# Products of zeros at the start, parameter loads on one queue, an earlier copy of the shift columns and a root on VectorE, in a one-layer decoder step

## The chip, the cores and the metric

One core of a Trainium2 chip runs the whole step. The metric is the device time of one execution in microseconds (us); the median of three runs counts. TensorE multiplies matrices, VectorE (DVE), ScalarE (ACT) and GpSimd (POOL) work on elements, and SyncE (SP) issues most of the transfers from and to device memory (HBM). Each engine takes its own instructions in order, and so does each queue of transfers.

## The reference, cut to what matters

One layer is computed for 512 prompt tokens and 8 sample tokens, 1024 wide, all in f32:

```
mod = silu(c) @ w_mod + b_mod              # six parts: sh1, sc1, g1, sh2, sc2, g2
h   = rmsnorm(x, norm1_g) * (1 + sc1) + sh1
u   = h @ w_in                             # q, f, i (v), output gate, x and y of the recurrence, two merge gates
o   = rmsnorm(hgrn2(q, f, v), hg_onorm_g) * silu(output gate)      # 8 heads of 128
b   = rglru(conv(x)) * gelu(y)
x   = x + g1 * ((sig(ga) * (o @ w_branch_a) + sig(gb) * (b @ w_branch_b)) @ w_out)
x   = x + g2 * (relu((rmsnorm(x, norm2_g) * (1 + sc2) + sh2) @ w_ff1) ** 2 @ w_ff2)
y   = rmsnorm(x, final_norm_g)
```

The prompt tokens share one conditioning vector; each of the 8 samples has its own, so there are 9 columns of `mod`. For the samples the recurrences take one step from stored states. The last two old inputs of the convolution (`state_conv`) are handed through to an output.

## The kernel before, in words

Activations lie transposed: 128 features in the partitions, 520 tokens (512 and 8) in the free dimension, cut into two halves of 260. A product of f32 precision is made of three products of the type fp32r: each operand is split into a high part (a cast on ScalarE) and a low part (a subtraction on VectorE), and TensorE adds high by high, high by low and low by high. A tile of weights is 128 columns by 1024 rows (512 KB); SP loads it (`_load_w`, L100), ScalarE casts `whi` (L113), VectorE subtracts `wlo` (L116), and for each of 8 blocks of rows TensorE makes six products of 128x260 (`gemm`, L155). Every two records of the trace on a plain f32 operand belong to one instruction.

**The opening** (`begin`, L1668) is written by hand, and a wrapper, `InOrder`, keeps TensorE, ScalarE and VectorE in the order of the code; its operations all show as L72. `load_parameters` (L254) loads `pm` (b_mod and norm gains) and `pl` (bounds and decays) by ScalarE's queue and `pa` (convolution, gate biases and old states, and the norm gain of the heads) by GpSimd's; the samples `xsr` come by ScalarE's queue too. SP loads, in this order, the conditioning `c`, the first quarter ("piece 0") of the part of `w_mod` that makes the scale sc1, x rows 0 and 1, two weight tiles, piece 1, x rows 2 and 3, the third weight tile, x rows 4 to 7, pieces 2 and 3, and then `w_rows`, the part of `w_mod` that makes the shift sh1. Each piece is multiplied by silu(c) (`pt<-wm,cT`), evicted by ScalarE (`modev`), turned into columns (`pt<-pick,modev`), and its two rows of h, still without norm and shift, are cast (`h`, high on ScalarE, low on VectorE) and multiplied by the first three tiles (f, q and output gate of head 0; `fhi`, `flo`). Meanwhile the squares of x are summed for the norm's root `rs`.

Near the end of the opening the shift columns `shp` are there. h is cast again, now with norm and shift: `high_again` and `low_again`, eight each. The three tiles that are already multiplied get the shift afterwards: `pw` is the product of `shp` with the raw weights (L1893, `pb<-wst,shp`), ScalarE copies it to `sw` (`shw<-pb`), three small products (`pt<-pick,shw`) turn it into the column `bias`, VectorE copies that to `shb`, and ScalarE and VectorE add it to the three evicted results `ma`. `evict(2)` multiplies the third result by `rs`. Behind this stands the first ordinary tile, v of head 0 (`gemm`, which is tied behind the three small products by `last_product`).

**After the opening** a scheduler orders each engine by a simulated timeline, priorities and tied pairs (`behind`). Heads, recurrences and gates follow, all fed by the h of the opening.

**The gates** come after eight plain tiles: products of sums of quarter matrices (`gate_product`, L874, products on L897), whose weights are split into `wgate` four forms ahead (L870, L871); results go to `gp` by a copy on ScalarE (L908). The same stretch holds the end of the heads. `heads_sample_out` (L669) normalizes the samples' heads: a product sums squares over the partitions, ScalarE copies it (L676), and `root` (L213) on GpSimd adds a constant and raises to the power -0.5; VectorE multiplies `os` by it (L678). GpSimd's queue also stores the last two heads' outputs (`oaT_d<-e`, L666) and loads gate weights (`gw`, L853) and the recurrences' outputs (`t<-obT_d`, L788). `load_ob` (L780) splits those `t` into `b` (cast on ScalarE L209, subtraction on VectorE L210).

Of the kernel before, what the change touches and what calls it, by code (L numbers as in the profile page):

```python
# [17 lines left out]
NB = 8  # L18
T = L + NB
HALF = T // 2  # L20
KO = D // 128
H = 8
# [3 lines left out]
EPS = 1e-6  # L26
# [8 lines left out]
FIRSTS = 3  # L35
# [44 lines left out]
class Kernel:  # L80
# [126 lines left out]
    def split(self, full, pool, tag):  # L207
# [2 lines left out]
        self.nc.vector.tensor_tensor(lo, full, hi.bitcast(F32), OP.subtract)  # L210
        return hi, lo

    def root(self, out, x, n):  # L213

        p = self.nc.gpsimd
        p.tensor_scalar(out, x, n * EPS, None, OP.add)  # L216
        p.tensor_tensor(out, out, self.halfc.to_broadcast(list(out.shape)), OP.pow)
# [36 lines left out]
    def load_parameters(self):  # L254

        self.pm = self.consts.tile([128, 72], F32, name="pm")
        self.nc.scalar.dma_start(self.pm, self.i["params_mod"])
        self.bmod, self.n1g, self.n2g = self.pm[:, 0:48], self.pm[:, 48:56], self.pm[:, 56:64]
        self.gcol = self.pm[:, 70:72]
        self.pl = self.start.tile([128, 16], F32, name="pl")  # L260
        self.nc.scalar.dma_start(self.pl, self.i["params_bound"])
        t = self.hc.tile([128, 313], F32, name="pa")
        self.nc.gpsimd.dma_start(t, self.i["params"])
        self.ong = self.hc.tile([128, 1], F32, name="ong")
        self.nc.gpsimd.tensor_scalar(self.ong, t[:, 0:1], 128.0 ** 0.5, None, OP.mult)
        self.cw = t[:, 1:33].rearrange("p (j k) -> p j k", j=4)
        self.cb, self.ba, self.bx = (t[:, 33 + 8 * j:41 + 8 * j] for j in range(3))
        self.h0 = t[:, 57:121].rearrange("p (b k) -> p b k", b=NB)
        self.cbuf = t[:, 121:313].rearrange("p (b j k) -> p b j k", b=NB, j=3)
# [399 lines left out]
    def heads_sample_out(self):  # L669
        nc = self.nc  # L670
        sq = self.sm.tile([128, H * NB], F32, name="sq64")
        osf = self.os.rearrange("p h b -> p (h b)")
        nc.scalar.activation(sq, osf, AF.Square)
        ps = self.pps.tile([128, 512], F32, name="ps")
        nc.tensor.matmul(ps[:, :64], self.ones_r.bitcast(F32), sq, start=True, stop=True)
        nc.scalar.copy(sq, ps[:, :64])  # L676
        self.root(sq, sq, 128)
        nc.vector.tensor_tensor(osf, osf, sq, OP.mult)  # L678
        nc.vector.tensor_tensor(osf, osf, self.ogs.rearrange("p h b -> p (h b)"), OP.mult)

# [92 lines left out]
    def rg_out(self):  # L773
        nc, o = self.nc, self.o
        nc.gpsimd.dma_start(o["xlast"], self.xlast.rearrange("p n w -> p (n w)"))
        nc.gpsimd.dma_start(o["hlast"], self.hlast.rearrange("p n w -> p (n w)"))
        nc.gpsimd.dma_start(o["conv_old"], self.i["state_conv"][0, :, 1:3])


    def load_ob(self):  # L780
# [887 lines left out]
    def begin(self):  # L1668


        plain = self.nc
        nc = self.nc = InOrder(self.tc)
        self.start = self.open_pool("start", 1)
        mm = lambda: self.pmm.tile([128, 2, 512], F32, name="mm")
        ps = lambda: self.pps.tile([128, 512], F32, name="ps")
        pt = lambda: self.ppt.tile([128, 512], F32, name="pt")
        pb = lambda: self.ppb.tile([128, 512], F32, name="pb")
        self.load_c()
        self.load_parameters()
        xsr, fs, fsh = (self.start.tile([128, KO, NB], F32, name=n) for n in ("xsr", "fs", "fsh"))  # L1680
        nc.scalar.dma_start(xsr.rearrange("p k b -> p (k b)"), self.i["xs"])
        self.xT = [self.slot(self.start, f"xT{k}", bufs=1) for k in range(KO)]
        keys, raw, pieces = [self.head_cols(0)[j] for j in (0, 1, 3)], [], []

        def load_wide(name, i):
            w = self.start.tile([128, KO, 256], F32, name="wm", bufs=4)
            nc.sync.dma_start(w.rearrange("p k n -> p (k n)"), self.i[name][i])
            return w

        def load_piece(i):  # L1690
            pieces.append(load_wide("w_piece", i))

        load_piece(0)
        self.load_x(0, 1)
        for key in keys[:2]:
            raw.append(self._load_w(key, self.wst))
        load_piece(1)
        self.load_x(2, 3)
        raw.append(self._load_w(keys[2], self.wst))
        self.load_x(4, 5, 6, 7)  # L1700
        load_piece(2)
        load_piece(3)

# [121 lines left out]
        p = self.piece(1, pieces[1])  # L1825
# [15 lines left out]
        p = self.piece(2, pieces[2])  # L1841
# [8 lines left out]
        rs = self.slot(self.start, "rs", bufs=1)  # L1850
# [3 lines left out]
        p = self.piece(3, pieces[3])  # L1854
# [29 lines left out]
        products(2, 6, 7, only=high_part)  # L1884
        self.mod_cols(0, self.shp[:, :, :NM], ev)
        products(2, 6, 7, only=low_parts)
        for i in range(KO // 2):
            high_again(2 * i, 2 * i + 1)
            low_again(2 * i, 2 * i + 1)
            samples_again(i)  # L1890
            if i == 0:
                evict(2)
        pw = pb()  # L1893
        for n in range(FIRSTS):
            for k in range(KO):
                r = 32 * (k % 4)
                nc.tensor.matmul(pw[r:r + 32, n * 128:(n + 1) * 128], self.shp[:, k, :], raw[n][:, k, :],
                                 start=k < 4, stop=k >= KO - 4)
        sw, b = self.start.tile([128, FIRSTS * 128], F32, name="shw"), self.start.tile([128, FIRSTS, 16], F32, name="shb")
        nc.scalar.copy(sw, pw[:, :FIRSTS * 128])  # L1900
        bias = pt()
        for n in range(FIRSTS):
# [4 lines left out]
            nc.scalar.activation(u[:, :L], u[:, :L], AF.Identity, bias=b[:, n, 0:1])  # L1907
            nc.vector.tensor_tensor(u[:, L:], u[:, L:], b[:, n, 1:9], OP.add)
        self.first = [self.two(u) for u in us]
        self.last_product = nc.tensor.last  # L1910
        self.nc = plain
        self.close_pool()
        nc = plain
# [144 lines left out]
```

## Time and profile before

| | |
|---|---|
| median of 3 runs | 1016.55 us (1015.34 to 1017.27) |
| the profiled execution | 1017.95 us, its span 1016.2 us |
| busy: TensorE, VectorE, ScalarE, GpSimd | 97%, 68%, 52%, 14% of the span |
| HBM read, written | 123.65 MB, 11.26 MB |

Times in the views are microseconds from the start of the span. A row of the timeline gives the start, the length, the engine (PE is TensorE's products, PEld its weight loads, a q behind a name its queue), the line, the operation, out<-in, shapes and count, and in brackets the idle time before it with what ended it. A row of the waits gives who waited for whom, the microseconds in total, how often, and the longest. A row of the windows gives the stretch, its length, the busy time of PE, PEld, DVE, ACT and POOL with their counts, the clock that TensorE was granted (1.00 is full), the busy share of the transfer engines and GB/s.

### The profile page before, as it was taken

What the parts mean: (1) busy time and instruction counts of PE and PEld (TensorE: products, weight loads), DVE (VectorE), ACT (ScalarE), POOL (GpSimd) and SP (SyncE); (2) the same over time, 40 slices, a digit from 0 to 9 for tenths busy, and PEclk for the clock granted to TensorE, in tenths of its full rate; (3) what the DMA queues carried; (4) which work ended last, traced back from release to release, by engine and by line L of the source; (5) the groups of instructions that cost most, each with busy time, mean ns of one, the idle gap of its engine ahead of it and who ended that gap; (6) DMA issues with size and microseconds to landing.
All of it is one profiled execution on the core that took longest, in us unless ns stands there. A gap on an engine that the chain in (4) does not pass through costs nothing. (4 is left out here: it accounts for less than half of the span.)

```text
span 1016.2 us, 23148 instructions
## 1 busy us (share of the span) xinstructions
PE 986.3 (97%) x9624; PEld 956.5 (94%) x9624; DVE 689.2 (68%) x1344; ACT 525.9 (52%) x998; POOL 146.3 (14%) x250
## 2 busy tenths in 40 slices
PE   6899999999999999979999999999999999999997
PEld 4799999999989999979999999999999999999996
DVE  6776766685685758858624546677767776778685
ACT  5554745725564573455512224466555645656662
POOL 1300000000000101161000000022321331232050
PEclk9989999999999999999999999999999999999998
DMA  9553353233234335335556665321662472273242
GB/s 364 199 180 115 114 163 116 103 126 128 97 126 154 113 100 197 109 106 199 175 203 243 225 244 187 97 91 48 152 176 63 97 197 102 55 179 80 64 84 85
DMA packets 48761, 143.67 MB, mean 141 GB/s; under 512 B 6240, under 2 KB 15776, under 8 KB 47624
## 3 DMA queue, kind: packets, MB, share of 16 engines
q1 hardware_dynamic: 36704, 123.23, 35.6%
q0 software_dynamic: 11504, 18.86, 8.3%
q8 instruction: 75, 1.23, 0.5%
q10 hardware_dynamic: 448, 0.11, 0.1%
q14 instruction: 30, 0.25, 0.1%
HBM read 123.65 MB, written 11.26 MB: 133 GB/s over the span
## 5 line engine op out<-in xcount | busy, mean ns | idle before, releaser
L155 PE MATMUL mm<-h,whi 128*128 128x260 f32 (+1 forms) x2720 | 453.1, 285 | 0.0
L155 PEld LDWEIGHTS mm<-h,whi 128*128 128x128 f32 x2720 | 380.0, 189 | 1.4 <-issue 0.8
L155 PE MATMUL mm<-h,wlo 128*128 128x260 f32 x1360 | 280.7, 286 | 2.6 <-DVE wlo L116 2.6
L116 DVE TENSOR_TENSOR wlo<-wst,whi 128x1024 fp32r<-128x1024 f32 x156 | 190.2, 1220 | 126.5 <-ACT whi L113 125.2
L113 ACT CAST whi<-wst 128x1024 fp32r<-128x1024 f32 x156 | 164.0, 1053 | 185.2 <-PE mm L155 145.0
L155 PEld LDWEIGHTS mm<-h,wlo 128*128 128x128 f32 x1360 | 213.0, 189 | 3.7 <-DVE wlo L116 3.2
L1280 POOL TENSOR_TENSOR ft<-ft,fsh 128x8 f32<-128x8 f32 x28 | 18.4, 658 | 209.2 <-DVE ft L1274 209.2
L1288 DVE TENSOR_TENSOR f<-f 128x260 f32<-128x260 f32 x64 | 27.3, 426 | 27.9 <-ACT f L1283 27.2
L1277 ACT ACTIVATE ft<-ft,fsh 128x512 f32<-128x512 f32 (+2 forms) x36 | 24.1, 678 | 36.0 <-DVE ft L1274 36.0
L155 PE MATMUL mm<-oa,whi 128*128 128x260 f32 x256 | 41.6, 284 | 0.0
L155 PE MATMUL mm<-b,whi 128*128 128x260 f32 x256 | 41.6, 284 | 0.0
L155 PE MATMUL mm<-a,whi 128*128 128x260 f32 x256 | 41.4, 284 | 0.0
L569 DVE TENSOR_TENSOR X<-X,tb 128x512 f32<-128x512 f32 x48 | 30.8, 680 | 11.0 <-PE ps L561 8.6
L216 POOL TENSOR_SCALAR ss<-ss 128x4 f32<-128x4 f32 x8 | 2.4, 304 | 246.7 <-ACT g L653 246.6
L155 PEld LDWEIGHTS mm<-oa,whi 128*128 128x128 f32 x256 | 34.8, 188 | 2.1 <-ACT whi L113 1.6
L155 PEld LDWEIGHTS mm<-b,whi 128*128 128x128 f32 x256 | 35.1, 188 | 1.7 <-ACT whi L113 1.2
L155 PEld LDWEIGHTS mm<-a,whi 128*128 128x128 f32 x256 | 35.0, 188 | 1.2 <-PE pt L346 0.8
L179 ACT ACTIVATE gate<-pb,pa 128x260 f32<-128x260 f32 x32 | 15.5, 486 | 32.1 <-PE pb L701 32.1
L1322 POOL DMA_DIRECT2D ma<-snap x28 | 26.4, 956 | 39.2 <-issue 30.7
L1304 POOL DMA_DIRECT2D ma<-snap x28 | 26.1, 932 | 39.2 <-DMA ma<-snap 23.8
L871 DVE TENSOR_TENSOR wgate<-gw,wgate 128x512 fp32r<-128x512 f32 x28 | 19.2, 690 | 15.0 <-ACT wgate L870 14.3
L1283 ACT ACTIVATE f<-ft 128x520 f32<-128x520 f32 (+1 forms) x36 | 20.8, 589 | 14.9 <-POOL ft L1281 12.9
(560 smaller groups left out, 2083.2 us busy)
## 6 DMA issues: line engine op xcount, KB each, us to landing
wst<-in_w_ff_dram SPq DMA_DIRECT2D x64, 512.0 KB, 3.9
wst<-in_w_in_dram SPq DMA_DIRECT2D x56, 512.0 KB, 3.5
wst<-in_w_mod_dram SPq DMA_DIRECT2D x32, 512.0 KB, 4.4
wm<-in_w_piece_dram SPq DMA_DIRECT2D x4, 1024.0 KB
wm<-in_w_rows_dram SPq DMA_DIRECT2D x4, 1024.0 KB, 12.0
st<-in_state_hgrn_dram SPq DMA_DIRECT2D x8, 512.0 KB, 4.1
vb<-vd SPq DMA_DIRECT2D x8, 512.0 KB, 3.7
out_dram<-st SPq DMA_DIRECT2D x8, 512.0 KB
```

The lines of the kernel that those rows point to most:

```text
L113: ins = self.nc.scalar.copy(hi, st)
L116: self.nc.vector.tensor_tensor(lo, st, hi.bitcast(F32), OP.subtract)
L155: self.last_product = self.nc.tensor.matmul(ps[s][:, :c.stop - c.start], x, y[:, c], start=first and n == 0, stop=last and n == 2)
L179: ins = self.nc.scalar.activation(out, x, AF.Sigmoid, **kw)
L569: last = nc.vector.tensor_tensor(half, half, factors(tbs, x, b), OP.mult)
L871: nc.vector.tensor_tensor(lo, x, hi.bitcast(F32), OP.subtract)
L1277: nc.scalar.activation(t[:, :p], t[:, :p], AF.Relu, bias=sh[:, 0:1])
L1280: eng.tensor_tensor(t[:, p:], t[:, p:], sh[:, 1:9], OP.add)
L1283: nc.scalar.activation(f, self.two(self.ft)[:, a:a + n], AF.Square)
L1288: self.nc.vector.tensor_tensor(f[:, n], f[:, a], f[:, b], op)
L1304: nc.gpsimd.dma_start(x[1][:, b], v[:, :n], accum_op=OP.add)
L1322: nc.gpsimd.dma_start(x[t][:, a], s[p], accum_op=OP.add)
```

## The change

- Six f32 products of zeros (`shp`, just cleared) stand ahead of piece 0 on TensorE.
- `pm`, `pl` and `xsr` are issued by SP (the first two ahead of piece 0, `xsr` behind x row 1), and `pa` too, between x row 7 and piece 2. `ong`, which reads `pa`, is computed later in the code. The copy of `state_conv` to an output stands behind a late product instead of in the opening.
- The copy to `sw` stands behind the fourth `high_again` instead of behind the eighth; `evict(2)` stands behind all of them. The small products, `shb` and the additions are outside the wrapper now, and v's tile is tied to the last product of `pw`, not to the small ones.
- The samples' root is computed by VectorE: an integer estimate and three Newton steps, 12 operations, and one that reads the sum straight from PSUM.

```
     def load_parameters(self):
-        self.nc.scalar.dma_start(self.pm, self.i["params_mod"])
+        self.nc.sync.dma_start(self.pm, self.i["params_mod"])
...
-        nc.scalar.copy(sq, ps[:, :64])
-        self.root(sq, sq, 128)
+        nc.vector.tensor_scalar(sq, ps[:, :64], 128 * EPS, None, OP.add)
+        sq = self.rsqrt_small(sq, H * NB, w=H * NB)
...
+    def rsqrt_small(self, x, n, p=128, w=16):
...
+        nc.vector.tensor_scalar(t.bitcast(I32), x.bitcast(I32), 1, None, OP.arith_shift_right)
+        nc.vector.tensor_scalar(y.bitcast(I32), t.bitcast(I32), -1.0, float(0x5F3759DF), OP.mult, OP.add)
+        nc.vector.tensor_scalar(h, x, -0.5, None, OP.mult)
+        for _ in range(3):
+            nc.vector.tensor_tensor(t, y, y, OP.mult)
+            nc.vector.tensor_tensor(t, t, h, OP.mult)
+            nc.vector.scalar_tensor_tensor(y, t, 1.5, y, OP.add, OP.mult)
...
-        nc.gpsimd.dma_start(o["conv_old"], self.i["state_conv"][0, :, 1:3])
+        self.behind(nc.gpsimd.dma_start(o["conv_old"], self.i["state_conv"][0, :, 1:3]), self.last_product)
...
         self.load_parameters()
+        warm = pb()
+        for _ in range(6):
+            nc.tensor.matmul(warm[:, :256], self.shp[:, :4, :], self.shp, start=True, stop=True)
...
         self.load_x(4, 5, 6, 7)
+        nc.sync.dma_start(self.pa, self.i["params"])
         load_piece(2)
...
-        for i in range(KO // 2):
-            high_again(2 * i, 2 * i + 1)
-            low_again(2 * i, 2 * i + 1)
-            samples_again(i)
-            if i == 0:
-                evict(2)
         pw = pb()
...
-        nc.scalar.copy(sw, pw[:, :FIRSTS * 128])
+        for i in range(KO // 2):
+            high_again(2 * i, 2 * i + 1)
+            low_again(2 * i, 2 * i + 1)
+            samples_again(i)
+            if i == 1:
+                nc.scalar.copy(sw, pw[:, :FIRSTS * 128])
+        evict(2)
+        self.last_product = nc.tensor.last
+        self.nc = nc = plain
         bias = pt()
+        nc.gpsimd.tensor_scalar(self.ong, self.pa[:, 0:1], 128.0 ** 0.5, None, OP.mult)
...
-        self.last_product = nc.tensor.last
-        self.nc = plain
         self.close_pool()
```

On TensorE, at the end of the opening, the product of the shift with the raw weights (`pb<-wst,shp`) was followed by the three small products and then by v's tile (`whi` and `wlo` rows):

```order
L72 MATMUL pb<-wst,shp 32x128 x24
L72 MATMUL pt<-pick,shw 128x9 x3
L155 MATMUL mm<-h,whi 128x260 x4
L155 MATMUL mm<-h,wlo 128x260 x2
L155 MATMUL mm<-h,whi 128x260 x4
L155 MATMUL mm<-h,wlo 128x260 x2
```

Now it is followed by v's tile at once:

```order
L72 MATMUL pb<-wst,shp 32x128 x24
L155 MATMUL mm<-h,whi 128x260 x4
L155 MATMUL mm<-h,wlo 128x260 x2
L155 MATMUL mm<-h,whi 128x260 x4
L155 MATMUL mm<-h,wlo 128x260 x2
L155 MATMUL mm<-h,whi 128x260 x4
L155 MATMUL mm<-h,wlo 128x260 x2
L155 MATMUL mm<-h,whi 128x260 x2
L1923 MATMUL pt<-pick,shw 128x9 x3
L155 MATMUL mm<-h,whi 128x260 x2
L155 MATMUL mm<-h,wlo 128x260 x2
```

The three small products moved into the fourth of v's eight blocks. On ScalarE the same place read, before (`h<-xT,shp` are the casts of `high_again`, `whi` the second ordinary tile's high part, `ma` the additions of the bias):

```order
L72 ACTIVATE h<-xT_124,shp 128x512
L72 ACTIVATE h<-xT_125,shp 128x512
L72 ACTIVATE h<-xT_126,shp 128x512
L72 ACTIVATE h<-xT_127,shp 128x512
L72 ACTIVATE h<-xT_128,shp 128x512
L113 CAST whi<-wst 128x1024
L72 COPY shw<-pb 128x384
L72 ACTIVATE ma<-ma,shb 128x512 x3
```

and reads now:

```order
L72 ACTIVATE h<-xT_128,shp 128x512
L72 COPY shw<-pb 128x384
L72 ACTIVATE h<-xT_129,shp 128x512
L72 ACTIVATE h<-xT_130,shp 128x512
L72 ACTIVATE h<-xT_131,shp 128x512
L72 ACTIVATE h<-xT_132,shp 128x512
L113 CAST whi<-wst 128x1024
L1927 ACTIVATE ma<-ma,shb 128x512 x3
```

The copy of the shift moved ahead of four casts and of `whi`. On ScalarE at the first gates, where `gp` are results of gate products and `b` the recurrences' outputs, the order before was

```order
L870 CAST wgate<-gw 128x512 x3
L908 COPY gp<-mm 128x260
L908 COPY gp<-ps 128x260
L209 CAST b<-t 128x520 x4
L908 COPY gp<-mm 128x260
L870 CAST wgate<-gw 128x512
```

and is now

```order
L883 CAST wgate<-gw 128x512 x3
L921 COPY gp<-mm 128x260
L921 COPY gp<-ps 128x260
L209 CAST b<-t 128x520 x3
L921 COPY gp<-mm 128x260
L883 CAST wgate<-gw 128x512
L209 CAST b<-t 128x520
```

The fourth cast of `b` moved behind the third copy to `gp`; the copy to `sq` for the root is gone from ScalarE, and the two operations of the root are gone from GpSimd.

More of the change, by code (lines that the diff above doesn't have):

```diff
@@ L211, in split @@
         return hi, lo
+    def rsqrt_small(self, x, n, p=128, w=16):
+        nc = self.nc
+        y, t, h = (self.sm.tile([128, w], F32, name=f"rs{w}_{a}", bufs=2 if w == 16 else 1) for a in "yth")
+        y, t, h = y[:p, :n], t[:p, :n], h[:p, :n]
+        nc.vector.tensor_scalar(t.bitcast(I32), x.bitcast(I32), 1, None, OP.arith_shift_right)
[5 more added lines that the diff above has]
+            nc.vector.scalar_tensor_tensor(y, t, 1.5, y, OP.add, OP.mult)
+        return y
     def root(self, out, x, n):
@@ L260, in load_parameters @@
         self.pl = self.start.tile([128, 16], F32, name="pl")
-        self.nc.scalar.dma_start(self.pl, self.i["params_bound"])
-        t = self.hc.tile([128, 313], F32, name="pa")
-        self.nc.gpsimd.dma_start(t, self.i["params"])
+        self.nc.sync.dma_start(self.pl, self.i["params_bound"])
+        self.pa = t = self.hc.tile([128, 313], F32, name="pa")
         self.ong = self.hc.tile([128, 1], F32, name="ong")
-        self.nc.gpsimd.tensor_scalar(self.ong, t[:, 0:1], 128.0 ** 0.5, None, OP.mult)
         self.cw = t[:, 1:33].rearrange("p (j k) -> p j k", j=4)
@@ L1679, in begin @@
         self.load_parameters()
+        warm = pb()
+        for _ in range(6):
+            nc.tensor.matmul(warm[:, :256], self.shp[:, :4, :], self.shp, start=True, stop=True)
         xsr, fs, fsh = (self.start.tile([128, KO, NB], F32, name=n) for n in ("xsr", "fs", "fsh"))
-        nc.scalar.dma_start(xsr.rearrange("p k b -> p (k b)"), self.i["xs"])
         self.xT = [self.slot(self.start, f"xT{k}", bufs=1) for k in range(KO)]
@@ L1694, in begin @@
         self.load_x(0, 1)
+        nc.sync.dma_start(xsr.rearrange("p k b -> p (k b)"), self.i["xs"])
         for key in keys[:2]:
@@ L1899, in begin @@
         sw, b = self.start.tile([128, FIRSTS * 128], F32, name="shw"), self.start.tile([128, FIRSTS, 16], F32, name="shb")
-        nc.scalar.copy(sw, pw[:, :FIRSTS * 128])
+        for i in range(KO // 2):
[7 more added lines that the diff above has]
+        self.nc = nc = plain
         bias = pt()
-        for n in range(FIRSTS):
+        nc.gpsimd.tensor_scalar(self.ong, self.pa[:, 0:1], 128.0 ** 0.5, None, OP.mult)
+        for n, u in enumerate(us):
             nc.tensor.matmul(bias[:, 16 * n:16 * n + NM], sw[:, n * 128:(n + 1) * 128], self.pick[:, :NM], start=True,
@@ L1909, in begin @@
         self.first = [self.two(u) for u in us]
-        self.last_product = nc.tensor.last
-        self.nc = plain
         self.close_pool()
-        nc = plain
         pool = lambda name, **kw: self.tc.tile_pool(name=name, bufs=2, reuse_waits="tile", **kw)
```

## The prediction, made before the changed kernel had run

> **What bounds the kernel now.** TensorE is the bound: the page has it busy for 97% of the span, so I first asked the waits of TensorE what it waited for, up to 52 us and behind that:
>
> ```profile
> PE pt L72 <- DMA wm<-in_w_piece_dram: 6.9, 1, 6.9
> PE pt L72 <- ACT shw L72: 4.2, 1, 4.2
> ...
> PE mm L897 <- ACT gp L908: 5.5, 2, 4.4
> PE mm L155 <- DVE wlo L116: 2.6, 3, 0.9
> ```
>
> Three waits matter: for the first piece, for the copy of the shift (`shw`) and for a gate copy (`gp`). The change touches each of them. Then I asked the windows for the granted clock around them:
>
> ```profile
> 12.18:15.60 3.42, 3.12 (x12) 2.68 (x12) 3.42 (x4) 2.44 (x4) 0.00 (x0) 1.00 1.00 392
> 46.32:49.73 3.41, 0.95 (x36) 0.68 (x28) 3.41 (x7) 3.41 (x7) 3.06 (x8) 1.00 0.59 173
> 53.14:56.56 3.42, 3.42 (x17) 3.42 (x17) 1.19 (x6) 3.36 (x6) 0.00 (x0) 0.50 0.65 229
> 56.56:60.00 3.44, 3.44 (x31) 3.44 (x30) 3.44 (x14) 2.67 (x9) 0.00 (x0) 1.00 0.83 314
> 298.86:302.27 3.41, 2.48 (x21) 2.33 (x20) 3.41 (x7) 2.50 (x4) 0.00 (x0) 1.00 0.66 197
> 455.95:459.36 3.41, 3.41 (x24) 1.91 (x23) 2.79 (x6) 3.41 (x7) 0.26 (x1) 0.50 0.46 125
> 1005.50:1008.90 3.40, 2.34 (x18) 2.16 (x18) 2.53 (x13) 1.10 (x3) 0.41 (x2) 1.00 0.27 94
> 1008.90:1012.00 3.10, 1.22 (x12) 0.75 (x10) 2.25 (x6) 1.55 (x3) 0.00 (x0) 0.50 0.48 190
> ```
>
> The clock changes only at these borders, which lie a multiple of 3.41 us apart. It falls to 0.50 behind a window in which TensorE was busy for 0.95 of 3.41 us or 2.34 of 3.40, and stays at 1.00 through one of 2.48 of 3.41; so the limit is near 70% busy. It comes back behind a window that was busy throughout. A wait of 4 us therefore costs twice: itself, and half of the work up to the next border but one.
>
> **Products of zeros, and the parameters.** The timeline of the opening:
>
> ```profile
> 6.92 1.93 PE L72 MATMUL pt<-wm,cT 128*32 128x256 f32 x16 [6.92 <-DMA wm<-in_w_piece_dram]
> 7.00 0.17 DVE L72 COPY ptmp<-pl 128x8 f32<-128x8 f32 x1 [2.76 <-DMA pl<-in_params_bound_dram]
> 9.93 1.05 ACT L72 CAST fhi<-wst 128x1024 fp32r<-128x1024 f32 x1 [0.26 <-DMA wst<-in_w_in_dram]
> 11.28 1.34 ACT L72 ACTIVATE h<-xT,modT 128x512 fp32r<-128x512 f32 x2 [0.30 <-DVE modT L72]
> 12.05 2.28 PE L72 MATMUL mm<-h,fhi 128*128 128x260 f32 x8 [1.31 <-ACT h L72]
> 14.64 1.24 PE L72 MATMUL mm<-h,flo 128*128 128x260 f32 x4 [0.30 <-DVE flo L72]
> 20.28 1.12 PE L72 MATMUL ps<-h,fhi 128*128 128x260 f32 x8
> 24.95 1.07 PE L72 MATMUL pt<-wm,cT 128*32 128x256 f32 x16
> 27.71 0.22 POOL L72 TENSOR_TENSOR fs<-xsr,modT 128x16 f32<-128x16 f32 x1 [5.29 <-DVE modT L72]
> 33.88 1.05 PE L72 MATMUL pb<-rsd,ones_r 128*128 128x128 f32 x8
> ```
>
> The first windows are marked 1.00, but the same eight products last 2.28 us at 12.05 and 1.12 at 20.28, and a piece 1.93 and 1.07: the opening runs at half speed. The window up to 15.60 (3.12 of 3.42 us busy) did not end that; the one up to 19.01 did.
>
> Cost of the six: four f32 products of 128 columns take 1.05 us at full speed, 0.26 each, so one of 256 columns takes 0.26 to 0.53, at half speed 0.53 to 1.05, six 3.2 to 6.3 us. `shp` is cleared at about 1.4 us, so they end between 4.6 and 7.7 us, beside the wait for piece 0. I take no cost; the latest end would cost 0.8 us, were it not for the next point.
>
> Gain: `pm` and `pl` go ahead of piece 0 on SP, each one issue (some 0.4 us), so piece 0 comes up to 0.8 us later; `pa`, `xsr` and the state copy no longer run beside it, which gives part of that back. I take 7.3 us. `pl` came at 7.00 and had held VectorE for 2.76 us; it now comes before piece 0, and ScalarE's exponentials and table load with it. But next in line on ScalarE is the cast of `fhi`, which waits at 9.93 for its tile, whose bytes are no fewer ahead of it. So h starts at 11.0 instead of 11.28, and the first real products at 11.8 instead of 12.05: 0.25 us. Between piece 0 (over at 8.4 if at full speed) and 11.8 TensorE has only the two column products, half a microsecond. Every 3.41 us window that covers this hole is busy for 55% at most, under the 70% limit, wherever its borders fall. So even if the six products lift the clock, I expect it to lapse before the stream, and to come back near 19 us as before, give or take half a window of 3.41 us at half speed, 0.9 us. The term is -0.2, bounds -2.1 (clock held: the chain reaches 14.4 us on ScalarE and VectorE as before, and from there 4.6 us to 19.0 run at full speed, less 0.2 for waits) and +0.9.
>
> [...]
>
> `pa` now lies between x row 7 and piece 2. Its reader `ong` stands on GpSimd ahead of the sample step of 27.71. Piece 2, next behind it, was in use at 24.95 with no wait shown, so `pa` is there in time; if not, each microsecond past 27.7 delays the samples' columns of h and TensorE alike. I take 0. The state copy moves to a stretch behind the gates where GpSimd only issues loads: 0.
>
> **The shift.** The timeline there:
>
> ```profile
> 45.10 5.03 ACT L72 ACTIVATE h<-xT,shp 128x512 fp32r<-128x512 f32 x8 [0.99 <-DVE shp L72]
> 45.76 1.52 PE L72 MATMUL pb<-wst,shp 128*32 128x128 f32 x48
> 47.20 0.76 DVE L72 TENSOR_TENSOR ma<-ps,rs 128x260 f32<-128x260 f32 x2
> 47.87 4.06 DVE L72 SCALAR_TENSOR_TENSOR h<-xT,shp,h 128x512 fp32r<-128x512 f32 x6
> 50.97 0.47 ACT L72 COPY shw<-pb 128x384 f32<-128x384 f32 x1
> 51.49 1.45 PE L72 MATMUL pt<-pick,shw 128*128 128x9 f32 x6 [4.22 <-ACT shw L72]
> 52.79 1.21 PE L155 MATMUL mm<-h,whi 128*128 128x260 f32 x4
> 58.16 0.65 PE L155 MATMUL mm<-h,whi 128*128 128x260 f32 x4
> 58.88 0.65 PE L155 MATMUL mm<-h,whi 128*128 128x260 f32 x4
> 60.33 0.65 PE L155 MATMUL mm<-h,whi 128*128 128x260 f32 x4
> ```
>
> TensorE is through with `pw` at 47.28, waits 4.2 us for a copy behind eight casts, does the small products (51.49 to 52.79) and v's eight blocks (to 60.33, the next tile), up to 56.56 at half speed: 13.05 us. Now v follows at once. A block takes 0.72 us at full speed (58.16 to 58.88), eight 5.76; the small products half of 1.30, 0.65; together 6.4, to 53.7 us. What is late next: block k needs `low_again` k. VectorE goes on at 47.28 with rows 2 to 7 at 0.68 each, `evict(2)` (0.76) now behind them; ScalarE has a cast each 0.63, 0.47 later from row 4 on. So row 2 is ready at 47.9, needed at 48.7; row 7, behind `shb`, at 51.7, needed at 53.0. The second tile's `whi` ends near 51.6; its `wlo` (1.2 us, behind `evict(2)`) near 53.9, as it is needed. The third tile's `whi` stands behind the bias and four sigmoid passes, near 57, its `wlo` near 60.2 for 60.0. I charge 0.3 for that. Gain 13.05 - 6.4 - 0.3 = 6.3; bounds 4 (each of these ends a microsecond later) and 6.7.
>
> **The samples' root.** GpSimd, ScalarE, VectorE and TensorE at the gates:
>
> ```profile
> 438.46 10.55 POOL L217 TENSOR_TENSOR sq<-sq,halfc 128x64 f32<-128x64 f32 x1
> 448.96 1.18 POOL L666 DMA_DIRECT2D oaT_d<-e  x2
> ...
> 446.20 1.69 ACT L209 CAST b<-t 128x520 fp32r<-128x520 f32 x3
> 452.73 0.63 ACT L209 CAST b<-t 128x520 fp32r<-128x520 f32 x1 [4.83 <-DMA oaT_d<-e]
> 453.26 0.37 ACT L908 COPY gp<-mm 128x260 f32<-128x260 f32 x1
> ...
> 441.71 0.69 DVE L665 TENSOR_TENSOR e<-pb,e 128x512 f32<-128x512 f32 x1 [0.47 <-PE pb L663]
> 449.05 0.23 DVE L678 TENSOR_TENSOR os<-os,sq 128x64 f32<-128x64 f32 x1 [2.56 <-POOL sq L217]
> ...
> 447.63 1.61 PE L897 MATMUL pb<-h,wgate 128*128 128x260 f32 x12
> 453.68 2.97 PE L897 MATMUL mm<-a,wgate 128*128 128x260 f32 x12 [4.45 <-ACT gp L908]
> ```
>
> The power takes 10.55 us on GpSimd. Behind it wait the stores of `e`, issued at 448.96 though `e` was ready at 442.4; ScalarE's fourth `b` waits for them until 452.73 (`b` takes over that memory), and behind `b` stands the copy to `gp` for which TensorE waits 4.45 us. Then it runs at half speed from 453.68 to 459.36: another 2.84. Together 7.3.
>
> Now VectorE has 13 operations on 128x64; `os` shows 0.23 for one, so 3.0 us, among the `wgate` splits and ahead of the second `e`. If all of it delayed that `e`, it would end at 445.4, the stores go out then, and 3.8 us later (448.96 to 452.73, as before) the fourth `b` can start. That `b` now stands behind the `gp` copy, which comes after three casts of `b`, at 447.9 + 0.4 = 448.3, before TensorE ends its product at 449.24. So the wait goes. What is late next is the loads of the fifth and sixth `t` ahead of a later copy on ScalarE; I charge 0.5. Gain 6.8; bounds 2.5 (a wait over 1 us remains and the clock falls again) and 7.3.
>
> **The sum.** -0.2 - 6.3 - 6.8 = -13.3 us. Against the profiled execution (1017.95, span 1016.2 and 1.75 around it) that is 1004.65. The median of the runs is 1016.55, 1.4 lower, and their spread of 1.9 us is what borders 3.41 us apart would make of three slow stretches; so I put the sum on the median: 1003.2.
>
> **Rivals.** (1) The clock holds across the hole of the opening. For it: the six products fill the time up to piece 0. Against it: the 70% limit. Then -2.1 for -0.2: 1001.3. [...] Chance 0.12.
>
> (2) The gate wait shrinks but stays over 1 us, with ScalarE behind the later `t` loads, and the clock falls again: 1 to 2 us and 2.8. For it: ScalarE takes everything in one order and a fifth `t` needs the buffer of the first. Against it: TensorE needs that later copy only some 8 us after. 1003.2 + 4.3 = 1007.5. Chance 0.20.
>
> (3) Slower: up to the second pair of heads the order of all engines is laid out anew, over some 20 tiles, and `wlo` comes late for them, since ScalarE and VectorE lose the slack that TensorE's wait for `shw` had given them. Its price is the longest such wait, 0.9 us a tile. It decides from 15 tiles on (13.3 / 0.9); all 20 give 1003.2 + 18.0 = 1021.2. Against it: before, only three waits on `wlo` are shown behind 52 us, 2.6 us. Chance 0.03.
>
> (4) The gains are eaten further on by transfers that come no sooner than before, and nothing is left: 1016.5. Against it: of TensorE's waits the views show only the first piece's as one for a load. Chance 0.02.
>
> My forecast has the remaining 0.63: 1003.2, its own range 1001.5 to 1005.5. The range that leaves out about 2 in 10 goes from 1000.5 (rival 1 with 0.8 for the borders) to 1008 (rival 2). A measurement here tells 0.2%, 2 us, from no change: faster 0.95, within 0.2% 0.02, slower 0.03.
>
> **What would show it.** Right: no wait of TensorE on `shw`, v's first `whi` right behind `pb<-wst,shp`, the clock at 1.00 from there to the gates, no power on GpSimd at 64 columns, no wait over 1 us on L921's `gp`. The opening: eight `h,fhi` products of about 2.3 us mean it lapsed, 1.1 that it held. Wrong: a new wait of TensorE over 1 us anywhere behind 50 us, or a window under 70% busy there.

## The result and the profile after

The changed kernel takes 1006.66 us in the median of four runs (1005.01 to 1007.33), the kernel before 1016.91 us beside it (1015.34 to 1017.46): ratio 0.9899, 95% interval 0.9882 to 0.9916. That is 10.2 us faster, where the forecast had 13.3 us and 1003.2 us; the time lies in the range, near the price of rival 2 (1007.5). The profiled execution took 1007.33 us, its span 1005.5 us; against 1016.2 us before, 10.7 us less. The 2.6 us between 13.3 and 10.7 are what had to be found.

The waits of TensorE in the changed kernel, up to 52 us and behind that (who waited for whom: us in total, times, longest):

```profile
PE mm L72 <- ACT h L72: 2.2, 1, 2.2
PE pb L72 <- DVE shp L72: 1.5, 1, 1.5
PE pt L72 <- DVE ptmp L325: 1.0, 1, 1.0
...
PE mm L155 <- DVE wlo L116: 2.6, 3, 1.0
PE mm L72 <- DVE ma L72: 1.2, 1, 1.2
PE mm L910 <- DVE wgate L884: 1.2, 1, 1.2
PE mm L910 <- ACT gp L921: 1.0, 1, 1.0
PE mm L910 <- ACT wgate L883: 1.0, 1, 1.0
```

The waits on `shw` (4.2 us) and the long one on `gp` (4.4 us) are gone. What is new are two waits on `wgate`, the split gate weights: 1.0 us for ScalarE's cast and 1.2 us for VectorE's subtraction. The wait of 1.0 us on `gp` is the smaller of the two that stood there before. The windows around the half-speed stretches of the changed kernel (length, busy time of PE, PEld, DVE, ACT, POOL, clock, share of the transfer engines, GB/s):

```profile
7.29:10.70 3.41, 1.68 (x20) 1.02 (x20) 1.24 (x8) 0.50 (x2) 0.01 (x1) 1.00 1.05 419
10.70:14.12 3.42, 1.82 (x7) 1.72 (x8) 1.84 (x3) 3.42 (x5) 0.62 (x3) 0.50 1.01 409
14.12:17.53 3.41, 3.10 (x23) 1.68 (x21) 2.45 (x3) 0.74 (x2) 0.00 (x0) 0.50 1.04 398
451.02:454.44 3.42, 1.81 (x12) 1.59 (x13) 2.68 (x5) 1.14 (x3) 0.53 (x1) 1.00 0.02 5
454.44:457.85 3.41, 3.41 (x18) 3.41 (x17) 1.23 (x3) 1.43 (x4) 0.00 (x0) 0.50 0.49 154
```

The clock lapses in the opening's hole and comes back at 17.5 us; from there it stays at 1.00 through the shift and up to 454.4 us, and falls at the gates, behind the window that holds the two waits on `wgate`. (Near the end of the kernel it falls at 1000.6 us, as it did at 1008.9 us before.)

To see where the time went, the span is cut at three places that every trace has: the start of the shift product (`pb<-wst,shp`), the first gate product (`mm<-h,wgate`) and the first product of `b` (`mm<-b,whi`). These are the rows of TensorE's timeline in the changed kernel:

```profile
45.32 1.52 PE L72 MATMUL pb<-wst,shp 128*32 128x128 f32 x48
46.77 0.74 PE L155 MATMUL mm<-h,whi 128*128 128x260 f32 x4
434.79 1.60 PE L910 MATMUL mm<-h,wgate 128*128 128x260 f32 x12
484.05 0.40 PE L155 MATMUL mm<-b,whi 128*128 128x260 f32 x2
```

And in the kernel before, whose shift product starts at 45.76 us (a row of the prediction):

```profile
441.99 1.62 PE L897 MATMUL mm<-h,wgate 128*128 128x260 f32 x12
460.39 3.04 PE L897 MATMUL mm<-h,wgate 128*128 128x260 f32 x24
494.40 0.40 PE L155 MATMUL mm<-b,whi 128*128 128x260 f32 x2
```

| | before | after | difference | forecast |
|---|---|---|---|---|
| opening, to the shift product | 45.76 | 45.32 | -0.44 | -0.2 |
| shift and heads, to the first gate product | 396.23 | 389.47 | -6.76 | -6.3 |
| gates, to the first product of `b` | 52.41 | 49.26 | -3.15 | -6.8 |
| rest, to the end of the span | 521.80 | 521.45 | -0.35 | 0 |

The difference is in one term: the gates. TensorE's rows there, in the changed kernel:

```profile
445.92 3.04 PE L910 MATMUL mm<-h,wgate 128*128 128x260 f32 x24
448.80 1.61 PE L910 MATMUL ps<-a,wgate 128*128 128x260 f32 x12
451.42 0.52 PE L910 MATMUL mm<-a,wgate 128*128 128x260 f32 x2 [1.00 <-ACT wgate L883]
453.15 1.53 PE L910 MATMUL mm<-a,wgate 128*128 128x260 f32 x10 [1.22 <-DVE wgate L884]
454.48 2.80 PE L910 MATMUL pb<-h,wgate 128*128 128x260 f32 x12
```

The same `x24` row, at 445.92 us here, starts at 460.39 us in the kernel before. So up to here the change had brought 14.47 us, all that the three terms promised (14.1 without the charge of 0.5 and the stall of 0.3). Then 2.2 us go to two new waits and 1.5 us to half speed (2.80 us for twelve products that take 1.61 at full speed, and 1.95 for 1.60 in the next row): 3.7 us.

### The profile page after: what moved, and what is told of

The parts are those of the page before. It is cut to its first block, busy times and chain, and to the rows that moved or that the text cites. A ratio compares the mean times of both kernels' runs of the same rounds, so it can differ in the third digit from the quotient of the medians.

```text
span 1005.5 us, 23181 instructions
## 1 busy us (share of the span) xinstructions
PE 985.9 (98%) x9636; PEld 956.4 (95%) x9636; DVE 689.7 (69%) x1357; ACT 524.4 (52%) x997; POOL 136.7 (14%) x247
## 5 line engine op out<-in xcount | busy, mean ns | idle before, releaser
L155 PE MATMUL mm<-a,wlo 128*128 128x260 f32 x128 | 25.8, 283 | 0.0
```

The source lines that it names most:

```text
L155: self.last_product = self.nc.tensor.matmul(ps[s][:, :c.stop - c.start], x, y[:, c], start=first and n == 0, stop=last and n == 2)
```

## The experiments

Three theories for the new wait: **A**, VectorE is late because of the root's own 3.0 us; **B**, ScalarE stands 2.2 us for the load of the fifth `t`, and the `wgate` casts behind it are late (the forecast's rival 2); **C**, VectorE has more to do between 442 and 453 us than fits, because the splits of `b` stand there among those of `wgate`, and before most of them were done while TensorE stood still or ran at half speed. In the kernel before, six of the eight lie between 449.45 and 459.4 us; TensorE stood from 449.24 to 453.68 us and ran at half speed up to 459.36. The first two of them:

```profile
449.45 1.30 DVE L210 TENSOR_TENSOR b<-t,b 128x520 fp32r<-128x520 f32 x2
```

The rows for B (ScalarE) and C (VectorE's groups from 442.0 to 453.6 us: busy time, mean ns of one | idle before) in the changed kernel:

```profile
442.63 0.42 ACT L179 ACTIVATE gp<-gp 128x260 f32<-128x260 f32 x1
445.28 1.30 ACT L209 CAST b<-t 128x520 fp32r<-128x520 f32 x2 [2.23 <-DMA t<-obT_d]
```

```profile
L884 DVE TENSOR_TENSOR wgate<-gw,wgate 128x512 fp32r<-128x512 f32 x7 | 4.6, 684 | 0.0
L210 DVE TENSOR_TENSOR b<-t,b 128x520 fp32r<-128x520 f32 x5 | 3.5, 696 | 0.7 <-ACT b L209 0.7
L879 DVE TENSOR_TENSOR gw<-gw 128x512 f32<-128x512 f32 x4 | 2.7, 685 | 0.0
L923 DVE TENSOR_TENSOR gp<-pb,gp 128x260 f32<-128x260 f32 x1 | 0.4, 430 | 0.5 <-PE pb L910 0.5
```

In these 11.6 us VectorE is idle for 1.2 us at most. All of the root's operations are over at 436.5 us.

**The shift alone** (`shift_only`): the kernel before with

```
+        for i in range(KO // 2):
...
+            if i == 1:
+                nc.scalar.copy(sw, pw[:, :FIRSTS * 128])
+        evict(2)
+        self.last_product = nc.tensor.last
```

> The kernel before with the shift's part of the change alone (copy to `shw` behind the fourth cast, small products outside the wrapper, v tied to the last product of `pw`). If the shift's gain is its own, as the trace of after says (v's tile and all behind it 6.7 us earlier, beside 0.44 us from the opening), the ratio to before is 0.9934, -6.7 us; the forecast's term of -6.3 would be 0.9938. The gates keep their wait of 4.45 us on `gp` and a stretch at half speed. Rival: the gain needs the other parts (VectorE and ScalarE lose their slack and the tiles behind the opening wait for `wlo`, or the borders of the clock at the gates fall worse): -4 us or less, 0.996 or more.

Measured: ratio 0.9944 (0.9932 to 0.9956), 5.7 us faster (4.5 to 6.9). In its trace the stretch from the shift product to the first gate product takes 389.75 us, 6.5 less than before; the gates take 52.03, with their wait of 4.5 us. The shift's gain is its own.

**The root alone** (`root_only`): the kernel before with

```
-        nc.scalar.copy(sq, ps[:, :64])
-        self.root(sq, sq, 128)
+        nc.vector.tensor_scalar(sq, ps[:, :64], 128 * EPS, None, OP.add)
+        sq = self.rsqrt_small(sq, H * NB, w=H * NB)
```

> The kernel before with the samples' root on VectorE alone. Theory A, the root moves its cost to the gates by itself: it takes away 7.3 us (4.45 of waiting, 2.84 at half speed) and brings the wait on `wgate` of some 2.2 us and about 1.5 us at half speed that after shows: -3.6 us, ratio 0.9965. Rival: that new wait comes of the shift's or the opening's part (another order behind them) and is not there: -7.0 us, ratio 0.993.

Measured: 0.9962 (0.9948 to 0.9976), 3.9 us faster. The gates take 48.59 us, and the new wait is there without any other part of the change:

```profile
459.24 0.50 PE L912 MATMUL mm<-a,wgate 128*128 128x260 f32 x2 [1.00 <-ACT wgate L885]
460.32 2.05 PE L912 MATMUL mm<-a,wgate 128*128 128x260 f32 x10 [0.58 <-DVE wgate L886]
462.17 2.59 PE L912 MATMUL pb<-h,wgate 128*128 128x260 f32 x12
```

Together they are 1.6 us here, for 2.2 in the changed kernel. So the wait comes with the root's move, not with the new order behind the shift. Which of A, B and C is behind it this run can't say.

**No Newton steps** (`no_newton`): after with

```
-        for _ in range(3):
+        for _ in range(0):
```

> After without the three Newton steps (the samples' root is left at its integer estimate): 9 operations of 0.22 us, 2.0 us, are off VectorE ahead of the gates. Theory A, VectorE has more to do there than fits, the root's 3 us and eight splits of `b` among those of `wgate`: the wait of TensorE on `wgate` at the gates falls from 2.2 us to 0.3 or less, no window is under 70% busy, the clock holds; 3.4 us faster than after, ratio 0.9865. Theory B, the cause is the loads of the fifth to eighth `t`, for which ScalarE stands 2.2 us and the `wgate` casts and splits behind it are late: `t` comes some 1 us earlier at the most, the wait stays over 1 us and the clock falls again; ratio 0.989 to 0.990.

Measured: 0.9888 (0.9876 to 0.9901). Both waits are what they were:

```profile
450.99 0.50 PE L910 MATMUL mm<-a,wgate 128*128 128x260 f32 x2 [1.01 <-ACT wgate L883]
452.71 1.48 PE L910 MATMUL mm<-a,wgate 128*128 128x260 f32 x10 [1.23 <-DVE wgate L884]
```

Two microseconds less work on VectorE, nine of the root's operations, and the waits are no shorter: A is out. The clock held here, though (1.00 from 446.0 to 456.4 us), and the gates take 47.72 us; the last run takes this up.

**Only four loads** (`four_loads`): after with

```
-            t = self.slot(self.tail, "t", bufs=4)
-            self.nc.gpsimd.dma_start(t, self.obT_d[n])
+            if n < 4:
+                ts.append(self.slot(self.tail, "t", bufs=4))
+                self.nc.gpsimd.dma_start(ts[n], self.obT_d[n])
+            t = ts[n % 4]
```

> After with only four of the eight loads of `t` in the gates' stretch: the fifth to eighth `b` are split once more from the first four `t`, so half of `b` is a copy of the other half. ScalarE and VectorE do the same work in nearly the same order; only the wait of 2.2 us of ScalarE for the fifth `t` can't occur. Theory B (the loads set it): TensorE's waits on `wgate` of 1.0 and 1.2 us go or fall under 0.5 together, and with them any stretch at half speed there; 2.2 to 3.4 us faster than after, ratio 0.986 to 0.988. Rival (VectorE and ScalarE have simply more splits than fit between TensorE's products, with or without the loads): both waits stay near 1 us, ratio 0.9885 to 0.990.

Measured: 0.9884 (0.9869 to 0.9899), the gates 47.46 us. ScalarE doesn't stand for a load any more; TensorE waits all the same, 2.0 us for 2.2:

```profile
443.05 1.66 ACT L209 CAST b<-t 128x520 fp32r<-128x520 f32 x3
```

```profile
452.02 0.51 PE L913 MATMUL mm<-a,wgate 128*128 128x260 f32 x2 [1.50 <-ACT wgate L886]
452.98 1.49 PE L913 MATMUL mm<-a,wgate 128*128 128x260 f32 x10 [0.46 <-DVE wgate L887]
```

B is out. The time alone, between what B and its rival had, would not have told it, since the clock held in this trace (1.00 from 446.0 to 455.4 us). The same trace bears on ScalarE's casts of `b` too: they are over at 446.3 us, and ScalarE then stands twice for TensorE, 1.41 us and, ahead of the casts that TensorE waits for, 0.55 us:

```profile
445.64 0.62 ACT L209 CAST b<-t 128x520 fp32r<-128x520 f32 x1
450.55 0.38 ACT L924 COPY gp<-ps 128x260 f32<-128x260 f32 x1 [0.55 <-PE ps L913]
```

VectorE is busy without a gap from 442.2 to 452.9 us there. So it isn't the casts of `b` that fill ScalarE; whether its order, with that copy ahead of the casts of `wgate`, has a share in the first wait is not shown.

**`b` on GpSimd** (`b_pool`): after, for the last five of the eight `b`, with

```
-            self.ob.append(self.split(t, self.abb, "b"))
...
+            self.nc.scalar.copy(hi, t)
+            self.nc.gpsimd.tensor_tensor(lo, t, hi.bitcast(F32), OP.subtract)
```

> After with the subtraction for the low part of the last five `b` on GpSimd; their loads and ScalarE's casts stay where they are. VectorE is rid of 3.4 us (five times 0.69) between 442 and 453 us. Theory C (VectorE has more than it can do there: the splits of `b` among those of `wgate`, once TensorE no longer stands for 4.45 us): the waits on `wgate` of 1.0 and 1.2 us go or fall below 0.4 together, the stretch from the first gate product to the first one of `b` takes 45.0 to 45.5 us for after's 49.26, ratio 0.986 to 0.987. Rival: it is ScalarE, whose casts of `b` stand ahead of those of `wgate`: the waits stay at 2 us together, 47.5 to 49.2 us, ratio 0.9885 to 0.990. GpSimd's subtractions could also hold back its loads of `gw`; then TensorE waits for a `wgate` behind `gw` later than 455 us.

Measured: 0.9887 (0.9874 to 0.9901), the gates 46.41 us, with the clock held (1.00 from 445.0 to 454.4 us; 47.68 in a trace of the changed kernel in which it held, the last run below). The two waits fall to 0.25 and 0.66 us, 0.9 together for 2.2. That is the direction of C, but not the whole of it, and the groups of VectorE from 436 to 460 us show why:

```profile
L890 DVE TENSOR_TENSOR wgate<-gw,wgate 128x512 fp32r<-128x512 f32 x14 | 12.3, 897 | 1.4 <-ACT wgate L889 1.2
L885 DVE TENSOR_TENSOR gw<-gw 128x512 f32<-128x512 f32 x8 | 6.2, 778 | 0.0
```

The same splits of `wgate` now take 897 ns in the mean for 688: VectorE was rid of 3.4 us and lost 3.7 us to slower operations (14 times 0.21 and 8 times 0.09), though part of that behind the wait. In place they look like this, beside the subtraction on GpSimd from 442.70 to 444.02 us:

```profile
442.68 2.51 DVE L890 TENSOR_TENSOR wgate<-gw,wgate 128x512 fp32r<-128x512 f32 x2
```

```profile
442.70 1.32 POOL L807 TENSOR_TENSOR b<-t,b 128x520 fp32r<-128x520 f32 x1
```

Two operations take 2.51 us, 1.2 us more than two in a row in the changed kernel (1.29), nearly the length of GpSimd's. Beside GpSimd's two from 446.10 to 449.63 us single operations on VectorE take 1.22 and 1.47 us; at 453.77 us, clear of any, one takes 0.68. What makes them slower is not shown.

**`b` spread out** (`b_spread`): after with each `b` tied behind a gate product, from the sixth on behind every second:

```
+            if s in range(6, 6 + 2 * KO, 2):
+                steps.append(([], self.load_b, (s - 6) // 2))
...
+        self.behind(self.nc.scalar.copy(hi, t), self.last_product)
```

> After, with the eight loads and splits of `b` tied behind the gate products 6, 8, ... 20, one behind every second, where after has them all among the first ten. All of the work is still done. Theories A and B both have it that the waits on `wgate` go (A: VectorE gets 5.5 us of `b` splits out of the crowd; B: the casts of `wgate` no longer stand behind a `b` that waits for its load): 3.8 us faster than after, ratio 0.986. If the wait is one of the gates' own (gate weights `gw` that are loaded late, sums and splits of `wgate` slower than TensorE's products even without `b`), it stays, ratio 0.990; and if `b` is then late for the first product of the next part, TensorE waits there instead, 0.988 or more.

Measured: 1003.8 us, 0.9873 (0.9861 to 0.9886). No wait on `wgate` is left, the gates take 44.95 us (4.3 less than after, 2.7 less than in the trace of the changed kernel whose clock held), the clock holds (1.00 from 446.0 to 455.4 us):

```profile
450.51 1.62 PE L914 MATMUL ps<-a,wgate 128*128 128x260 f32 x12
451.97 1.60 PE L914 MATMUL mm<-a,wgate 128*128 128x260 f32 x12
453.40 1.61 PE L914 MATMUL pb<-h,wgate 128*128 128x260 f32 x12
```

All of the work is done, only later. With A and B out and `b_pool` halfway, this leaves C: the crowd of `b` among `wgate` on VectorE. This run moved ScalarE's casts of `b` as well, so it can't part the two engines by itself; `four_loads` and `b_pool` speak for VectorE, and neither gives the full 2.2 us to it.

**The opening.** Three runs, without the six products, with more of them, and with the parameters on their old queues.

`no_zeros`: after without

```
-        for _ in range(6):
-            nc.tensor.matmul(warm[:, :256], self.shp[:, :4, :], self.shp, start=True, stop=True)
```

> After without the six products of zeros. Piece 0 then runs at half speed (1.9 us for 1.07) and its columns are 0.9 us later at the most; h has waited for the cast of `fhi` until 11.5 us in any case, 1.4 us behind the columns, so I expect the same time as after within 0.4 us, ratio 0.990, and the first real products at 12.3 us as before the removal. Rival: the zeros bring the clock's return forward (17.6 us in after), and without them it comes at 19 us or later: 0.7 us slower, ratio 0.9906.

Measured: 0.9903 (0.9889 to 0.9918), not to be told from after. Piece 0 takes 1.93 us for 1.07, and the first real products start at 12.28 us for 12.30.

`queues_back`: after with `pm`, `pl`, `xsr` on ScalarE's queue and `pa` on GpSimd's:

```
-        self.nc.sync.dma_start(self.pm, self.i["params_mod"])
+        self.nc.scalar.dma_start(self.pm, self.i["params_mod"])
```

> After with the loads of `pm`, `pl` and `xsr` on ScalarE's queue and `pa` on GpSimd's again, at the start, as in the kernel before. After's trace shows the cast of `fhi` at 10.57 us, before's at 9.93, and h at 11.53 and 11.28; if the parameters on SyncE's queue hold back the first tile, the cast comes back to 9.9 us, h to 11.3 and the first products to 12.05, and the time is 0.2 to 0.4 us shorter than after's, ratio 0.9896. Rival: by the forecast the move gains 0.25 us, and undoing it costs that, ratio 0.9902, with `pl` again at 7 us and piece 0's columns behind it. Both are within what five rounds can tell by the time; the rows of the trace decide.

Measured: 0.9897 (0.9881 to 0.9914), not to be told from after either. The cast of `fhi` starts at 10.26 us, for 10.57 in the changed kernel's first profile; but in the five other traces with the changed kernel's opening it starts between 9.77 and 10.16. So what the queues cost or bring is below what single traces tell, and stays open.

`fill`: after with five more products of zeros,

```
         split_first(0)
+        zeros(1)
         self.piece_cols(p)
+        zeros(4)
```

> After with five more products of zeros in the hole of the opening: one between piece 0 and its two column products, four behind those. If the clock lapses in after because the windows around the hole are too little busy, it now holds: the first eight products take 1.1 us for 2.3, piece 1 0.8 for 1.5, and the clock stays at 1.00 from about 7 us on. They start no later than 12.3 us. Behind 14.8 us (low part of the first tile, VectorE) the gain is what the half-speed products lost: 0.7 at piece 1 and about as much up to 17.5 us. I expect 1.2 us faster than after, ratio 0.9887; rival (a): VectorE and ScalarE pace the stream there whatever TensorE's clock, 0 to 0.4 us, ratio 0.9896 to 0.990; rival (b): the clock lapses all the same, the products still last 2.3 us, and the time is that of after or 0.4 longer.

Measured: 1005.36 us, 0.9885 (0.987 to 0.99), 1.3 us less than after; the intervals overlap, and the changed kernel's second median (1005.0, the last run) is as low, so the time shows no gain. In its trace the clock is at 1.00 from 15.3 to 21.0 us and 0.999 in the mean of the span; the low part of the first tile and piece 1 run at full speed (0.75 and 1.07 us for 1.24 and 1.78), and the shift product starts at 44.18 us, the earliest of all runs. The first eight products do not take the 1.1 us expected:

```profile
11.57 1.96 PE L72 MATMUL mm<-h,fhi 128*128 128x260 f32 x8 [0.39 <-ACT h L72]
```

Up to 14.2 us, where TensorE waits 0.63 us for `flo`, ScalarE and VectorE pace the stream, as rival (a) has it, and what the held clock brings comes behind that. Counted from ScalarE's first cast of `h`, whose start differs from trace to trace, the shift product comes after 33.4 us here, after 33.6 in `no_zeros`, after 33.8 to 34.5 us in five of the six traces with the changed kernel's opening, and after 36.2 in the sixth (`b_spread`, where the clock came back only at 22.9 us). So what the held clock brings is mostly some tenths of a microsecond.

**Together** (`both`: `b_spread` and `fill`; `both_tied`: with the order at the first gate product mended as well):

```
+        if s - 5 in self.gate_copy:
+            self.behind(ins, self.gate_copy[s - 5])
```

> After with both of the edits that paid: the five products of zeros in the opening's hole and the eight `b` spread over the gate products. If the two gains are independent, the time is after's less 2.9 us (`b` spread, median 1003.8 beside 1006.7) and less 1.3 us (the hole filled, 1005.4): 1002.5 us, ratio 0.9859. By the stretches of the traces it could be more, since the run with `b` spread had the clock come back only at 22.9 us in its opening: opening as in the run with the hole filled (`pb<-wst,shp` at 44.2 us), gates from the first product to the first one of `b` 44.95 us as in the run with `b` spread, end as in all: a span of 1000.1, a time of 1001.8, ratio 0.985. Rival: the filled hole only moves the wait and the gain of the one is part of the other's; 1003.8, ratio 0.987.

> The same with one more edit: the cast of a `wgate` stands behind the copy to `gp` of the gate product five places earlier, so that the copy of the first gate product isn't behind a cast that waits 0.81 us for TensorE. If the wait of 1.04 us of TensorE on `gp` comes of that order, it falls to 0.3 us or less, and the time is 0.8 us shorter than without the edit, ratio lower by 0.0008. Rival: the bank is needed back as soon as the product in between is over and the copy can't be earlier; no difference.

Measured: `both` 1002.19 us, 0.9854 (0.984 to 0.9867); `both_tied` 1001.62 us, 0.9845 (0.9832 to 0.9858). `both` is near the 1002.5 of two independent gains and below the rival's 1003.8, whose ratio of 0.987 lies just outside the interval; the last edit takes the wait on `gp` away, though its 0.6 us are within the noise of the times. The gates take 44.94 and 43.66 us. The products of zeros don't always hold the clock: in `both_tied` it fell at 14.8 us all the same, behind this window, which begins just where they end, and came back at 18.2:

```profile
11.38:14.79 3.41, 2.25 (x12) 1.64 (x12) 3.10 (x4) 2.89 (x5) 0.00 (x0) 1.00 1.00 401
```

What TensorE still waits for behind 40 us in `both_tied`:

```profile
PE mm L155 <- DVE wlo L116: 2.6, 3, 0.9
PE mm L72 <- DVE ma L72: 1.2, 1, 1.2
PE ps L570 <- DVE X L586: 0.8, 3, 0.3
```

This version beats both kernels: 15.7 us below the one before, 5.0 and 3.4 below the changed one's two medians (1006.66, and 1005.0 in the next run).

**The changed kernel once more** (`after_again`), no edit.

> The changed kernel once more, for a second profile. If the half-speed stretch at the gates is a matter of where the borders of the clock's windows happen to fall, TensorE's three waits there are again 1.0, 1.0 and 1.2 us, and the stretch from the first gate product to the first one of `b` takes either 49.2 us again (one window holds both later waits) or 47.5 us (a border parts them), and the start of `pb<-wst,shp` lies anywhere from 44.9 to 47.1 us; from there to the first gate product 389.5 us in both cases. If the waits fix it, 49.2 us and a start within 0.2 us of 45.3. Median 1006.5, ratio 0.9897.

Measured: 1005.0 us, 0.9889 (0.987 to 0.9908), and a span of 1003.1 us for 1005.5. The same program, the same waits, and no half speed at the gates (47.68 us for 49.26):

```profile
450.47 0.51 PE L910 MATMUL mm<-a,wgate 128*128 128x260 f32 x2 [0.95 <-ACT wgate L883]
452.20 1.49 PE L910 MATMUL mm<-a,wgate 128*128 128x260 f32 x10 [1.22 <-DVE wgate L884]
453.53 1.60 PE L910 MATMUL pb<-h,wgate 128*128 128x260 f32 x12
```

Its border at 450.36 us (an estimate: 160 windows of 3.413 us before the fall of the clock at 996.5 us; 290 such windows lie between the falls at 10.70 and 1000.57 in the first profile) leaves 0.1 us of the first wait in the window of the second; in the first profile the border at 451.02 leaves 0.4 us there, and the clock fell. So 1.6 us at the gates differ between two executions of one program; that the border decides it is a reading of these two profiles, which no run shows by itself.

## Why the prediction was right, and where it was off

**Size.** Faster by over 0.2% came true, and 1006.66 us is inside 1000.5 to 1008.0, but 3.5 us above the number: 2.6 us of it in the traces, the rest the difference between profiled executions and medians.

**The opening: right, with no meaning in the decimals.** The six products cost and bring nothing that the times tell (`no_zeros`), they did not hold the clock, the eight products took 2.28 us, and it came back at 17.5 us. The reason given, windows under 70% busy, is borne out by the window of 1.68 in 3.41 us, though 70% as a limit is not (last section). Piece 0 came at 7.94 for 7.3 us forecast, h at 11.53 for 11.0, later than the 11.28 before; in the five other traces with this opening h came between 10.72 and 11.11. For a clock that holds the forecast had -2.1 us; in `fill`, where it held, the shift product starts 1.6 us earlier than before. The -0.44 measured is not a gain of the change: in six traces with this opening the shift product starts between 44.55 and 47.08 us, in three with the old one between 45.63 and 47.10. `pa` and the state copy cost nothing: no wait for them is shown.

**The shift: right.** 6.4 us were forecast from the end of `pw` to the next tile, and v's eight blocks with the small products among them take from 46.77 to 53.28 us, 6.5 (the next tile's second block starts at 54.00, a block is 0.72). The 0.3 us charged for the third tile's `wlo` did not fall due: no wait between 46 and 60 us is shown. -6.76 for -6.3.

**The root: the removal right, the price wrong.** The power of 10.55 us is gone, the stores of `e` are issued at 434.34 for 448.96 us (7.2 us of that come from the two stretches ahead), and the 7.3 us of waiting and half speed behind it went in full. The step that failed is the next one: "What is late next is the loads of the fifth and sixth `t` ahead of a later copy on ScalarE; I charge 0.5". It measured 3.7 us (2.2 of new waits and 1.5 of half speed), or 2.2 where the clock holds, and the loads are not its cause (`four_loads`). In place of it stands VectorE, which the forecast had charged with the root's 3.0 us (no cost: `no_newton`) but not with work that was there all along. Before, six of its eight splits of `b` were done while TensorE stood for 4.45 us and ran at half speed; with that stretch gone, they crowd the splits of `wgate`. Both signs of being wrong that the forecast had named appeared there: a new wait over 1 us (1.22) and a window under 70% busy (1.81 of 3.42 us).

**The rivals.** Rival 2 had the outcome (a wait over 1 us stays, the clock falls again, 1007.5) with another mechanism: ScalarE behind `t`. The clock's fall there belongs to one of two profiles of the changed kernel: with the border at 451.02 us it fell, at 450.36 it held. Rivals 1, 3 and 4 did not occur: the clock did not hold across the hole; the waits on `wlo` are 2.6 us in all as before; the gains were not eaten by transfers.

## What to carry to other kernels

When a long wait of the bounding engine goes, list what the other engines did during it: that work now has to fit beside the engine at full speed, and an engine that is idle for hardly a moment there (VectorE here for 1.2 of 11.6 us) is the first to suspect of the next wait. To tell whose it is, take away one candidate's work at a time and read the wait, not the time; work taken away ahead of the last idle gap of that engine changed nothing here (`no_newton`). And spread work that isn't due yet over the stretch, instead of letting it run as soon as its data is there.

## What was not expected of the hardware

In these traces the limit of the clock is not one share of busy time. In the changed kernel's second profile, and in the run without Newton steps, it held behind these windows, 61% and 64% busy; before, it fell behind one of 2.34 in 3.40 us (69%):

```profile
450.36:453.77 3.41, 2.08 (x15) 1.87 (x16) 2.39 (x4) 0.90 (x4) 0.53 (x1) 1.00 0.10 14
```

```profile
451.17:454.58 3.41, 2.18 (x17) 1.98 (x17) 2.09 (x4) 0.91 (x4) 0.53 (x1) 1.00 0.12 28
```

It fell behind 1.81 of 3.42 us (53%). The window that fell at 69% held the small products at the end of the kernel, but the one of `both_tied` that fell at 2.25 of 3.41 us (66%) held ordinary ones of the first tile; what counts besides the share is not known. Nor did it take a full window to come back: 3.10 of 3.41 us (91%) did in the changed kernel, at 17.53 us, where 3.12 of 3.42 did not in the kernel before.

In `b_pool` VectorE's subtractions were slower beside GpSimd's (two took 2.51 us for 1.29; 897 ns for 688 in the mean of 14), so taking 3.4 us of them off it shortened TensorE's waits by 1.3 us only.
